# A tiled softmax on one core: unrolled instruction streams against loops with hand-placed semaphores

## The chip, the core and the metric

The kernel runs on one core of a Trainium2 chip. The metric is the device time of one execution in microseconds. Each execution also has a span, from the first to the last recorded instruction; in nearly all runs here the time is 1.7 to 1.8 us longer than the span. The granted clock was 1.0.

## The reference

```python
x = randn(32, 512, 1024) as float32; temperature = 0.5
scaled  = x / temperature
shifted = scaled - max(scaled, axis=-1, keepdims=True)
exp_x   = exp(shifted)
return exp_x / sum(exp_x, axis=-1, keepdims=True)
```

That is 16,384 rows of 1024 numbers. A tile is 128 partitions with 8 rows each, 4 MB, so there are 16 tiles. Everything is read once and written once: 67.11 MB each way.

## The kernel before

Each engine of the core has an instruction stream of its own; the page counts 224 busy instructions of DVE, 257 of ACT and 20 of Pool. SP (SyncE) issues the loads, DVE (VectorE) takes the maximum of a group of four rows and scales it into a bias, ACT (ScalarE) does the exponential and the sum of a row in one instruction of the program (in the trace an ACTIVATE of 1137 ns on the mean and an ACTIVATION_READ_ACCUMULATOR of 186 ns), DVE inverts the sums and multiplies the rows by them, and Pool (GpSimd) issues the store. A tile that was stored frees its buffer, one of six, for a new load. All is unrolled in Python: each engine gets a straight list of instructions, and the framework places the semaphores, the counters by which engines wait for one another. PE (TensorE) has nothing to do.

```python
TILES, BUFS, GROUP = [[8]] * 16, 6, 4
...
def maximum(g):       # DVE
    nc.vector.tensor_reduce(out=top, in_=tiles[i][:, a : a + k, :], axis=X, op=extreme)
    nc.vector.tensor_scalar_mul(bias, in0=top, scalar1=-scale)
def exponential(g):   # ACT, one instruction a row
    for b in range(k):
        nc.scalar.activation(row, row, Exp, bias=bias[:, b : b + 1], scale=scale, accum_out=sums[:, b : b + 1])
def divide(g):        # DVE
    nc.vector.reciprocal(recip, sums)
    for b in range(k):
        nc.vector.tensor_scalar_mul(row, in0=row, scalar1=recip[:, b : b + 1])
def store(g):         # Pool; then the next load, by SP
    nc.gpsimd.dma_start(out=dram(of, i)[...], in_=tiles[i][...])
    load()
...
for g in range(len(groups) + 1):      # a group's division comes after the next group's maximum
    if g < len(groups): maximum(g); exponential(g)
    if g > 0: divide(g - 1); store(g - 1)
```

Of the kernel before, what the change touches and what calls it, by code (L numbers as in the profile page):

```python
# [1 line left out]

# [4 lines left out]



TILES = [[8]] * 16  # L10
BUFS = 6

GROUP = 4


@with_exitstack
def kernel(
    ctx: ExitStack,
    tc: tile.TileContext,
    x: bass.AP,  # L20
    temperature: bass.AP,
    out: bass.AP,
):
    nc = tc.nc
    f32 = mybir.dt.float32
    scale = 1.0 / float(temperature)
    extreme = mybir.AluOpType.max if scale > 0 else mybir.AluOpType.min

    P = 128
    xf = x.flatten_outer_dims()  # L30
    of = out.flatten_outer_dims()
    n, d = xf.shape
    assert sum(sum(ks) for ks in TILES) * P == n

    data = ctx.enter_context(tc.tile_pool(name="data", bufs=BUFS))
    stats = ctx.enter_context(tc.tile_pool(name="stats", bufs=4))


    groups, first, r = [], [], 0
    for i, ks in enumerate(TILES):  # L40
        first.append(r)
        r += sum(ks)
        a = 0
        for k in ks:
            for b in range(0, k, GROUP):
                m = min(GROUP, k - b)
                groups.append((i, a + b, m, (a, k) if b + m == k else None))
            a += k

    def dram(t, i):  # L50
        k = sum(TILES[i])
        block = t[P * first[i] : P * (first[i] + k), :]
        return block.rearrange("(p k) d -> p k d", p=P, k=k)

    tiles, small = [], []

    def load():
        i = len(tiles)
        if i < len(TILES):
            xt = data.tile([P, sum(TILES[i]), d], f32, name="xt")  # L60
            nc.sync.dma_start(out=xt, in_=dram(xf, i))
            tiles.append(xt)

    def maximum(g):
        i, a, k, _ = groups[g]
        top, bias, sums, recip = (
            stats.tile([P, k], f32, name=name) for name in ("top", "bias", "sums", "recip")
        )
        small.append((bias, sums, recip))
        nc.vector.tensor_reduce(  # L70
            out=top, in_=tiles[i][:, a : a + k, :], axis=mybir.AxisListType.X, op=extreme
        )
        nc.vector.tensor_scalar_mul(bias, in0=top, scalar1=-scale)  # L73

    def exponential(g):
        i, a, k, _ = groups[g]
        bias, sums, _ = small[g]
        for b in range(k):
            nc.scalar.activation(  # L79
                tiles[i][:, a + b, :],  # L80
                tiles[i][:, a + b, :],
                mybir.ActivationFunctionType.Exp,
                bias=bias[:, b : b + 1],
                scale=scale,
                accum_out=sums[:, b : b + 1],
            )

    def divide(g):
        i, a, k, _ = groups[g]
        _, sums, recip = small[g]  # L90
        nc.vector.reciprocal(recip, sums)  # L91
        for b in range(k):
            nc.vector.tensor_scalar_mul(  # L93
                tiles[i][:, a + b, :], in0=tiles[i][:, a + b, :], scalar1=recip[:, b : b + 1]
            )

    def store(g):
        i, _, _, part = groups[g]
        if part:
            a, k = part  # L100
            nc.gpsimd.dma_start(out=dram(of, i)[:, a : a + k, :], in_=tiles[i][:, a : a + k, :])  # L101
            if a + k == sum(TILES[i]):
                load()



    with tc.manual_schedule():
        for _ in range(BUFS):
            load()
        for g in range(len(groups) + 1):  # L110
            if g < len(groups):
                maximum(g)
                exponential(g)
            if g > 0:
                divide(g - 1)
                store(g - 1)


# [1 line left out]
_INS = ['x', 'temperature']  # L120
_OUTS = [((32, 512, 1024), 'float32')]

_NUMBERS = {'temperature': 0.5}


# [26 lines left out]
```

## Time and profile before

| | before |
|---|---|
| time, median of 3 runs | 318.3 us (318.11 to 318.39) |
| the profiled run: time, span | 318.68 us, 316.9 us |
| instructions in the trace | 639 |
| DVE, ACT busy | 74%, 47% |
| packets of 32 KB on the DMA engines | 4096, that is 256 on each of 16 |
| instruction fetches of 8 KB inside the span | 4 |
| last byte written; semaphore of the last store; end of the span | 315.06; 315.45; 316.9 us |

How to read it: no compute engine is full, but the sixteen DMA engines are (loads 49.5% and stores 49.1% of their time), so the time of the run is the time of the DMA engine that finishes last (315.06 us) plus what follows it: 1.85 us to the end of the span and 1.8 us outside it.

### The profile page before, as it was taken

How to read it: one execution, taken by the hardware profiler on the slowest of the kernel's cores; microseconds unless marked ns; L12 is line 12 of the kernel's file. 1: busy time of each engine (PE TensorE's matmuls, PEld its weight loads, DVE VectorE, ACT ScalarE, POOL GpSimd, SP SyncE). 2: the span in 40 equal slices, each digit the busy share in tenths (PEclk: the TensorE clock that was granted, in tenths of full speed). 3: DMA queues.
4: the chain of work that ended last, by engine and by line, in shares of the span. 5: the costliest groups of instructions: out<-in, count | busy, mean ns of one | idle time of the engine just before them, and what ended most of it. 6: DMA issues, size and time to landing. Idle time of an engine off the chain costs nothing.

```text
span 316.9 us, 639 instructions
## 1 busy us (share of the span) xinstructions
DVE 235.5 (74%) x224; ACT 149.6 (47%) x257; POOL 8.8 (3%) x20
## 2 busy tenths in 40 slices
DVE  0399999999689494995949869496793967949710
ACT  0176666666526255361554606455163551635500
POOL 0000000000000000000000000000000000000000
DMA  8999999999999999999999999999999999999995
GB/s 331 409 451 414 385 459 422 438 436 422 455 405 455 409 459 405 455 422 438 434 426 451 409 455 411 455 414 447 426 434 435 426 451 409 451 418 447 430 414 232
DMA packets 4612, 134.25 MB, mean 424 GB/s; under 512 B 512, under 2 KB 512, under 8 KB 512
## 3 DMA queue, kind: packets, MB, share of 16 engines
q1 hardware_dynamic: 2304, 67.11, 49.5%
q0 software_dynamic: 2304, 67.11, 49.1%
q14 instruction: 4, 0.03, 0.0%
HBM read 67.11 MB, written 67.11 MB: 424 GB/s over the span
## 4 chain that ended last, share of the span: by engine, by line
issue 89%; DMA 4%; POOL 2%; POOLq 0%
DMA xt<-in_x_dram 4%; POOL out_dram L101 2%; POOLq L147 0%; POOLq L101 0%
## 5 line engine op out<-in xcount | busy, mean ns | idle before, releaser
L79 ACT ACTIVATE xt<-xt,bias 128x1024 f32<-128x1024 f32 x128 | 145.4, 1137 | 136.9 <-DVE recip L91 119.5
L70 DVE TENSOR_REDUCE top<-xt 128x4 f32<-128x4096 f32 x32 | 141.3, 4416 | 62.8 <-DMA xt<-in_x_dram 62.8
L93 DVE TENSOR_SCALAR xt<-xt,recip 128x1024 f32<-128x1024 f32 x128 | 87.7, 749 | 1.1
L79 ACT ACTIVATION_READ_ACCUMULATOR xt<-xt,bias 128x1 f32 x128 | 23.8, 186 | 0.0
L101 POOL DMA_DIRECT2D out_dram<-xt x16 | 8.6, 540 | 294.4 <-DVE xt L93 294.4
L79 ACT ACT_TABLE_LOAD x1 | 1.3, 1283 | 13.2 <-DMA xt<-in_x_dram 13.2
L91 DVE RECIPROCAL recip<-sums 128x4 f32<-128x4 f32 x32 | 5.5, 171 | 2.1 <-ACT xt L79 2.1
L73 DVE TENSOR_SCALAR bias<-top 128x4 f32<-128x4 f32 x32 | 5.4, 170 | 1.1
L133 POOL MEMSET const-float32-0.0<- 128x1 f32 x1 | 0.1, 98 | 0.2 <-issue 0.2
L133 POOL MEMSET const-bfloat16-1.0<- 128x1 bf16 x1 | 0.1, 101 | 0.0
L133 POOL MEMSET const-float32-1.0<- 128x1 f32 x1 | 0.1, 98 | 0.0
L133 POOL MEMSET const-uint8-127<- 128x1 uint8 x1 | 0.1, 98 | 0.0
## 6 DMA issues: line engine op xcount, KB each, us to landing
xt<-in_x_dram SPq DMA_DIRECT2D x16, 4096.0 KB, 50.2
out_dram<-xt POOLq DMA_DIRECT2D x16, 4096.0 KB, 38.4
```

The costliest lines, as they stand in the source:

```text
L70: nc.vector.tensor_reduce(out=top, in_=tiles[i][:, a : a + k, :], axis=mybir.AxisListType.X, op=extreme)
L73: nc.vector.tensor_scalar_mul(bias, in0=top, scalar1=-scale)
L79: nc.scalar.activation(tiles[i][:, a + b, :], tiles[i][:, a + b, :], mybir.ActivationFunctionType.Exp, bias=bias[:, b : b + 1], scale=scal ...
L91: nc.vector.reciprocal(recip, sums)
L93: nc.vector.tensor_scalar_mul(tiles[i][:, a + b, :], in0=tiles[i][:, a + b, :], scalar1=recip[:, b : b + 1])
L101: nc.gpsimd.dma_start(out=dram(of, i)[:, a : a + k, :], in_=tiles[i][:, a : a + k, :])
L133: nc = _bacc.Bacc("TRN2", target_bir_lowering=False, num_devices=1)
```

## The change

The intent was to cut the instruction lists of DVE and ACT to loops that need no fetching, and to tidy up both ends of the run: the first store is held until load 2 has landed, the last store goes by SP, and Pool need not be drained at the end.

```diff
-TILES = [[8]] * 16
-BUFS = 6
+SLOTS, ROWS = 6, 8
-GROUP = 4
+GROUPS = [4, 2, 2]
 ... (one ring of six slots in place of six tiles, one semaphore each for loaded and stored per slot)
+    def take(engine, sem, count=1):
+        engine.wait_ge(sem, count).then_inc(sem, -count)
 ...
+        for i in range(tiles):
+            nc.tensor.wait_ge(loaded[i % SLOTS], 16 * (i // SLOTS + 1)).then_inc(ready, 1)
+        nc.gpsimd.wait_ge(loaded[2], 16)
+        for i in range(tiles - 1):
+            nc.gpsimd.wait_ge(scaled, len(groups) * (i + 1))
+            nc.gpsimd.dma_start(out=dram(of, i), in_=slot(i)).then_inc(stored[i % SLOTS], 16)
+        with nc.vector.Fori(0, tiles) as t:
+            first = t % SLOTS * ROWS
+            take(nc.vector, ready)
+            for a, k in groups:          # all maxima of the tile
+                ... tensor_reduce, take(topped), tensor_scalar_mul, then_inc(biased, k)
+            for a, k in groups:          # then all its divisions
+                take(nc.vector, summed, k)
+                ... reciprocal, take(inverted), k products, then_inc(scaled, 1)
+        with nc.scalar.Fori(0, tiles) as t:
+            ... take(biased) at a group's first row; activation per row, then_inc(summed, 1)
+        nc.sync.wait_ge(scaled, len(groups) * tiles)
+        nc.sync.dma_start(out=dram(of, tiles - 1), in_=slot(tiles - 1)).then_inc(finished, 16)
 ... (both sections without the drain of Pool)
```

PE, which is idle otherwise, turns "load i has landed" into one counter, `ready`, for the loop of DVE. Since a loop's addresses depend on `t`, each row's instruction is preceded by a register step (128 on DVE and 128 on ACT), and each wait is an instruction of its own that also counts the semaphore down (160 on DVE, 48 on ACT). A first small activation (`warm`) makes ACT load its table earlier than at 13.2 us.

More of the change, by code (lines that the diff above doesn't have):

```diff
@@ L32 @@
     n, d = xf.shape
-    assert sum(sum(ks) for ks in TILES) * P == n
-    data = ctx.enter_context(tc.tile_pool(name="data", bufs=BUFS))
-    stats = ctx.enter_context(tc.tile_pool(name="stats", bufs=4))
-    groups, first, r = [], [], 0
-    for i, ks in enumerate(TILES):
-        first.append(r)
-        r += sum(ks)
-        a = 0
-        for k in ks:
-            for b in range(0, k, GROUP):
-                m = min(GROUP, k - b)
-                groups.append((i, a + b, m, (a, k) if b + m == k else None))
-            a += k
@@ L50, in dram @@
-    def dram(t, i):
-        k = sum(TILES[i])
-        block = t[P * first[i] : P * (first[i] + k), :]
-        return block.rearrange("(p k) d -> p k d", p=P, k=k)
-    tiles, small = [], []
-    def load():
-        i = len(tiles)
-        if i < len(TILES):
-            xt = data.tile([P, sum(TILES[i]), d], f32, name="xt")
-            nc.sync.dma_start(out=xt, in_=dram(xf, i))
-            tiles.append(xt)
-    def maximum(g):
-        i, a, k, _ = groups[g]
-        top, bias, sums, recip = (
-            stats.tile([P, k], f32, name=name) for name in ("top", "bias", "sums", "recip")
-        )
-        small.append((bias, sums, recip))
-        nc.vector.tensor_reduce(
-            out=top, in_=tiles[i][:, a : a + k, :], axis=mybir.AxisListType.X, op=extreme
-        )
-        nc.vector.tensor_scalar_mul(bias, in0=top, scalar1=-scale)
@@ L75, in exponential @@
-    def exponential(g):
-        i, a, k, _ = groups[g]
-        bias, sums, _ = small[g]
-        for b in range(k):
-            nc.scalar.activation(
-                tiles[i][:, a + b, :],
-                tiles[i][:, a + b, :],
-                mybir.ActivationFunctionType.Exp,
-                bias=bias[:, b : b + 1],
-                scale=scale,
-                accum_out=sums[:, b : b + 1],
-            )
-    def divide(g):
-        i, a, k, _ = groups[g]
-        _, sums, recip = small[g]
-        nc.vector.reciprocal(recip, sums)
-        for b in range(k):
-            nc.vector.tensor_scalar_mul(
-                tiles[i][:, a + b, :], in0=tiles[i][:, a + b, :], scalar1=recip[:, b : b + 1]
-            )
@@ L97, in store @@
-    def store(g):
-        i, _, _, part = groups[g]
-        if part:
-            a, k = part
-            nc.gpsimd.dma_start(out=dram(of, i)[:, a : a + k, :], in_=tiles[i][:, a : a + k, :])
-            if a + k == sum(TILES[i]):
-                load()
-    with tc.manual_schedule():
-        for _ in range(BUFS):
-            load()
-        for g in range(len(groups) + 1):
-            if g < len(groups):
-                maximum(g)
-                exponential(g)
-            if g > 0:
-                divide(g - 1)
-                store(g - 1)
+    tiles = n // (P * ROWS)
@@ new lines @@
+    assert tiles * P * ROWS == n and sum(GROUPS) == ROWS
+    groups = [(sum(GROUPS[:g]), k) for g, k in enumerate(GROUPS)]
+    of_group = dict(groups)
+    pool = ctx.enter_context(tc.tile_pool(name="data", bufs=1))
+    ring = pool.tile([P, SLOTS * ROWS, d], f32, name="ring")
+    top = pool.tile([P, ROWS], f32, name="top")
+    bias = pool.tile([P, ROWS], f32, name="bias")
+    sums = pool.tile([P, ROWS], f32, name="sums")
+    recip = pool.tile([P, ROWS], f32, name="recip")
+    warm = pool.tile([P, 1], f32, name="warm")
@@ new lines, with slot @@
+    loaded = [tc.alloc_semaphore(f"loaded{s}") for s in range(SLOTS)]
+    stored = [tc.alloc_semaphore(f"stored{s}") for s in range(SLOTS)]
+    ready, topped, biased, summed, inverted, scaled, finished = (
+        tc.alloc_semaphore(name)
+        for name in ("ready", "topped", "biased", "summed", "inverted", "scaled", "finished")
+    )
+    def dram(t, i):
+        return t[P * ROWS * i : P * ROWS * (i + 1), :].rearrange("(p k) d -> p k d", p=P, k=ROWS)
+    def slot(i):
+        s = i % SLOTS
+        return ring[:, ROWS * s : ROWS * (s + 1), :]
@@ new lines, in take @@
+    def take(engine, sem, count=1):
+        engine.wait_ge(sem, count).then_inc(sem, -count)
+    with tc.tile_critical(no_gpsimd_drain=True):
+        for i in range(tiles):
+            if i >= SLOTS:
+                nc.sync.wait_ge(stored[i % SLOTS], 16 * (i // SLOTS))
+            nc.sync.dma_start(out=slot(i), in_=dram(xf, i)).then_inc(loaded[i % SLOTS], 16)
+        for i in range(tiles):
+            nc.tensor.wait_ge(loaded[i % SLOTS], 16 * (i // SLOTS + 1)).then_inc(ready, 1)
[7 more added lines that the diff above has]
+            for a, k in groups:
+                nc.vector.tensor_reduce(
+                    out=top[:, a : a + k],
+                    in_=ring[:, bass.ds(first + a, k), :],
+                    axis=mybir.AxisListType.X,
+                    op=extreme,
+                ).then_inc(topped, 1)
+                take(nc.vector, topped)
+                nc.vector.tensor_scalar_mul(
+                    bias[:, a : a + k], in0=top[:, a : a + k], scalar1=-scale
+                ).then_inc(biased, k)
+            for a, k in groups:
+                take(nc.vector, summed, k)
+                nc.vector.reciprocal(
+                    recip[:, a : a + k], sums[:, a : a + k]
+                ).then_inc(inverted, 1)
+                take(nc.vector, inverted)
+                for b in range(a, a + k):
+                    row = ring[:, bass.ds(first + b, 1), :]
+                    ins = nc.vector.tensor_scalar_mul(row, in0=row, scalar1=recip[:, b : b + 1])
+                ins.then_inc(scaled, 1)
+        nc.scalar.activation(
+            warm, nc.const_aps.tensor(0.0, (P, 1)), mybir.ActivationFunctionType.Exp
+        )
+        with nc.scalar.Fori(0, tiles) as t:
+            first = t % SLOTS * ROWS
+            for b in range(ROWS):
+                row = ring[:, bass.ds(first + b, 1), :]
+                if b in of_group:
+                    take(nc.scalar, biased, of_group[b])
+                nc.scalar.activation(
+                    row,
+                    row,
+                    mybir.ActivationFunctionType.Exp,
+                    bias=bias[:, b : b + 1],
+                    scale=scale,
+                    accum_out=sums[:, b : b + 1],
+                ).then_inc(summed, 1)
+        i = tiles - 1
+        nc.sync.wait_ge(scaled, len(groups) * tiles)
+        nc.sync.dma_start(out=dram(of, i), in_=slot(i)).then_inc(finished, 16)
+        for i in range(tiles - SLOTS, tiles - 1):
+            nc.sync.wait_ge(stored[i % SLOTS], 16 * (i // SLOTS + 1))
@@ L120 @@
+    with tc.tile_critical(no_gpsimd_drain=True):
+        nc.sync.wait_ge(finished, 16, synchronizes=[nc.sync.lower_ap(slot(tiles - 1))])
 _INS = ['x', 'temperature']
```

## The prediction

> **What bounds the kernel now.** I read the page first: engines, DMA row, queues.
>
> ```profile
> span 316.9 us, 639 instructions
> DVE 235.5 (74%) x224; ACT 149.6 (47%) x257; POOL 8.8 (3%) x20
> ...
> DMA  8999999999999999999999999999999999999995
> ...
> q1 hardware_dynamic: 2304, 67.11, 49.5%
> q0 software_dynamic: 2304, 67.11, 49.1%
> q14 instruction: 4, 0.03, 0.0%
> ```
>
> No compute engine is full; the sixteen DMA engines are, in every slice but the first and the last: 49.5% + 49.1% of their time is packets of loads and stores. The trace's list of packets says how one engine spends its time: 16 loads and 16 stores of 4 MB are 4096 packets of 32 KB, 256 for each engine, and the usual packet takes 1.213 us. So an engine needs 256 x 1.213 = 310.5 us (16 x 32768 B / 1.213 us = 432 GB/s), and the first packet starts at 1.74 us. What can be won is only what an engine loses beside its 310.5 us, ahead of it and behind it.
>
> Then the end, in the view by windows (us, DVE, ACT, POOL, clock, DMA share, GB/s), the timeline and the view of the closing source line:
>
> ```profile
> 302.00:303.00 1.00, 0.60 (x1) 0.00 (x0) 0.10 (x1) 1.00 1.21 524
> 303.00:304.00 1.00, 0.00 (x0) 0.00 (x0) 0.43 (x1) 1.00 0.16 66
> 304.00:305.00 1.00, 0.00 (x0) 0.00 (x0) 0.00 (x0) 1.00 1.14 492
> ...
> 312.00:313.00 1.00, 0.00 (x0) 0.00 (x0) 0.00 (x0) 1.00 1.22 524
> 313.00:314.00 1.00, 0.00 (x0) 0.00 (x0) 0.00 (x0) 1.00 0.08 33
> 314.00:315.00 1.00, 0.00 (x0) 0.00 (x0) 0.00 (x0) 1.00 0.00 0
> ```
>
> ```profile
> 282.87 4.42 DVE L70 TENSOR_REDUCE top<-xt 128x4 f32<-128x4096 f32 x1 [4.48 <-DMA xt<-in_x_dram]
> ...
> 302.90 0.53 POOL L101 DMA_DIRECT2D out_dram<-xt  x1 [11.72 <-DVE xt L93]
> ```
>
> ```profile
> L147 SPq EVENT_SEMAPHORE  x11: 17/28/28, 315.5 to 316.8; - x11
> ...
> L147 POOLq DRAIN  x3: 34/101/13271, 302.9 to 316.6; - x3
> ```
>
> Two things stand there. Around 303.5 us most engines have finished store 14 and stand still up to 0.7 us, since the last store is issued at 302.90 and its first packet starts at 303.99. And a packet is counted where it starts: 33 GB/s in 313 to 314 is one packet of 32 KB, of one engine. Fifteen engines end by 314.2; this one starts its last packet at 313.84 and ends at 315.06. The store's semaphore is complete at 315.45, and the barriers take 1.46 us more, to 316.905. The late engine had no gap at 303: its last packet of store 14 ran to 305.38. So **the end is set by one engine that is behind the others**, and an earlier last store alone doesn't help it.
>
> Why is it behind? After each load's last packet every engine writes a 4-byte semaphore, and for one load to the next these lie 19.36 us apart, the same to 0.05 us on nearly every engine. The last engine's are 20.02 us apart twice: from 48.67 to 68.69 and from 223.63 to 243.65, +0.66 us each. The four packets of 8 KB on q14, instruction fetches, start at 64.4, 65.0, 193.9 and 241.8 us. Another engine loses some 0.5 us across the one at 193.9. The ACT waits carry the same mark:
>
> ```profile
> ACT xt L79 <- issue: 8.3, 3, 2.8
> ```
>
> [...] while both queues have work, a load takes 19.36 us, twice the 9.7 us that 8 packets take alone. [...] Here the fetch is hidden from ACT but costs its DMA engine 0.5 to 0.7 us. Whether a loop fetches again, no trace here shows. [...] Here 1.09 us for the last store by Pool, and 1.00 us for the first load by SP, so I count no gain from the path itself.
>
> **The change, part by part.**
>
> *Loops.* By the list of the built instructions the DVE program goes from 242 to 52 and ACT's from 177 (more as executed: the page counts 257 busy ones, since each activation also reads its accumulator) to 38. Both loops fit well inside what was fetched before the start, so the four fetches should go. The late engine gets 2 x 0.66 = 1.32 us back: its store 14 ends at 305.38 - 1.32 = 304.06 instead. The others finished store 14 between 303.3 and 304.15 (their semaphores). Eight more packets without a gap, 8 x 1.213 = 9.7 us, put the last byte at 313.0 to 313.8. I take 313.7 for the last, against 315.06: **-1.35 us**.
>
> *Order on DVE.* All maxima of a tile now come before its divisions, in groups 4, 2, 2. From a tile's landing: reduces 2 x 4.416 = 8.8 with three small operations 9.4 us. ACT starts at 4.6 and at 1.13 us a row has four rows at 9.3 and all eight at 13.9. DVE then has reciprocal and four products (0.66 apart) to 12.4, two rows to 14.0, the last two to 15.6. With semaphore hops and address registers I say 16.2 us, an estimate from these rows. Before, the last tile took 282.87 to 302.60, 19.7 us. So the last store is ready at 299.1, ahead of the 303.3 where the engines run dry: the gap at 303 goes. This is worth nothing added to the above; it is what keeps the other fifteen from becoming the new last ones (with the gap they end at 313.74 to 313.9). In the steady part DVE's 16.2 is under the 19.36 of DMA per tile.
>
> *First store waits for load 2.* Tile 0 is ready near 13.1 + 16.2 = 29.3, load 2 lands at 32.48; before, the first store went at 33.10. So it is issued 0.5 us earlier than before, which shifts the mix of loads and stores, not their sum: 0.
>
> *Last store by SP, and no Pool drain.* Pool's drain stood from 302.88 to 316.15, that is 0.70 us past the landing, but SP itself needed eight semaphore waits and two drains from 315.46 to 316.08, so the drain held up the barrier by 0.07 us. In the new program SP has about seven steps of 0.06 us after its wait on the last store, most other waits being done while the store runs. From landing to end 1.2 us instead of 1.46: **-0.25 us**.
>
> *Start.* One more hop between engines before SP's first load, some three steps: **+0.15 us**.
>
> Sum: -1.35 - 0.25 + 0.15 = -1.45; 318.3 - 1.45 = 316.85, say **316.8 us**.
>
> **Rivals.** (a) *The loops fetch at every jump back.* Fetches of 8 KB at 0.66 us of one engine, 16 rounds for DVE and ACT each: if they all hit one DMA engine, +10 to +20 us; spread evenly +1 to +2. [...] Against: the loop bodies are 38 and 22 instructions, and what stood resident at the start of before served at least 64 us. It would make 319 to 330. (b) *DVE becomes the bound.* Each dynamic address adds a register instruction (8 per tile and engine) and the semaphores are taken by instructions of their own, some 20 per tile on DVE. Slack is 19.36 - 16.2 = 3.2 us, so they would need 160 ns each, unhidden; the semaphore steps in the closing barrier lie 60 ns apart. Then 16 x the excess comes on top; at 200 ns each, +13 us. I think it unlikely. (c) *The lag comes back from elsewhere.* Packets of 1.5 to 2.4 us at the start and of 1.8 us around 36 us, where stores begin, are in both kernels; if the late engine's place came from them, only the end's 0.25 is left: 318.0. (d) *More is won*, because other engines' times at 303 hide losses too: the least conceivable is 1.74 + 0.8 for the slow first packet + 310.5 + 0.4 to the semaphore + 1.0 + 1.4 (318.3 - 316.9, time outside the span) = 315.8.
>
> **Range and chances.** Point (d) is nearly a floor, so faster by over 2% (under 311.9) is out of reach: 0.01. (c) gives the upper end of what I expect, 318.2. (a) and (b) together have 0.04 to pass 324.7. The rest, 0.95, is within 2%. Range 315.8 to 318.3.
>
> **What would show it.** q14 with no packets inside the span; every engine's load semaphores 19.36 us apart throughout; no window of low GB/s near 303; the last packets of all engines within some 0.9 us of each other, ending by 313.9; the last store issued by SP near 299; landing to end about 1.2 us. I am wrong if q14 still has packets (a), if DVE waits no longer for loads (b), or if one engine still ends a packet late without any fetch (c).

No term of the sum is among them: it stands at -1.35 - 0.25 + 0.15 = -1.45 and 316.85 us. Point (d) takes it that the steady part can't get faster; that is not shown. Of the 4096 packets of 32 KB none took less than 1.211 us, before or after. The 1.09 us of Pool's last store and the 1.00 us of SP's first load run from issue to first packet. Rival (a): against it, and for the step on loops, the trace of before has seven fetches of 8 KB on q14 between 10.5 and 7.4 us before the span and none from there to 64.4 us, when it has 47 instructions of DVE and 64 of ACT. And the 0.15 us for the start was an estimate.

## The result, and the profile after

| | before | after |
|---|---|---|
| median of 6 runs each, in the same rounds | 318.24 us (318.11 to 318.39) | 318.31 us (318.10 to 318.82) |
| ratio after / before, 95% interval | | 1.0005 (0.9992 to 1.0017): same |
| the profiled run: time, span | 318.68, 316.9 us | 318.14, 316.4 us |
| instructions in the trace | 639 | 1208 |
| 8 KB fetches inside the span | 4 | none |
| last byte; store's semaphore; end of span | 315.06; 315.45; 316.9 | 314.58; 315.06; 316.4 us |

A ratio is the mean time of one kernel's fast runs over the mean of the other's of the same rounds, so it is not quite the ratio of the medians quoted. The change moved nothing: the predicted 1.45 us did not come, and the median is just outside the range's upper end of 318.3.

The page of the changed kernel, in the parts that the prediction quoted of before (engines, DMA row, queues):

```profile
span 316.4 us, 1208 instructions
DVE 244.4 (77%) x272; ACT 148.1 (47%) x258; POOL 8.3 (3%) x19
...
DMA  8999999999999999999999999999999999999995
...
q1 hardware_dynamic: 2448, 71.30, 52.7%
q0 software_dynamic: 2160, 62.92, 46.1%
```

There is no line any more for q14, the queue of the instruction fetches: they are gone. The DMA row has not changed in a single digit. And the count of instructions has nearly doubled, though the programs became shorter. Of the 569 more, 354 are register steps and branches that a loop executes in every round (a_unrolled, below, has 854 without them); the rest are mostly the waits placed by hand and the smaller groups. The view by source line shows the waits alone, for the helper `take`:

```profile
L63 DVEq EVENT_SEMAPHORE  x160: 21/21/21, 13.4 to 296.7; - x160
L63 ACTq EVENT_SEMAPHORE  x48: 17/17/17, 18.5 to 291.9; - x48
```

These cost DVE and ACT almost nothing (21 and 17 ns each). The view of instruction groups says the same: before its maxima DVE still waits 39.4 us in all, for loads.

```profile
L84 DVE TENSOR_REDUCE top<-ring 128x2 f32 (+1 forms) x48 | 143.8, 2996 | 39.4 <-DVEq L63 39.4
```

The timeline of the last tile (start, duration, engine, line), and the view by windows (us, DVE, ACT, POOL, clock, DMA share, GB/s) of the end:

```profile
281.98 4.42 DVE L84 TENSOR_REDUCE top<-ring 128x4 f32 x1 [3.17 <-DVEq L63]
...
296.77 1.41 DVE L102 TENSOR_SCALAR ring<-ring,recip  x2 [0.15 <-DVEq L63]
298.21 0.35 SPq L127 DMA_DIRECT2D out_dram<-ring  x1
```

```profile
302.00:303.00 1.00, 0.00 (x0) 0.00 (x0) 0.00 (x0) 1.00 1.21 524
303.00:304.00 1.00, 0.00 (x0) 0.00 (x0) 0.00 (x0) 1.00 0.99 426
304.00:305.00 1.00, 0.00 (x0) 0.00 (x0) 0.00 (x0) 1.00 0.99 426
...
312.00:313.00 1.00, 0.00 (x0) 0.00 (x0) 0.00 (x0) 1.00 1.21 524
313.00:314.00 1.00, 0.00 (x0) 0.00 (x0) 0.00 (x0) 1.00 0.08 33
314.00:315.00 1.00, 0.00 (x0) 0.00 (x0) 0.00 (x0) 1.00 0.00 0
```

The last tile takes 281.98 to 298.18, 16.2 us instead of 19.7; the last store is issued at 298.21 rather than 302.90; the stretch of 66 GB/s near 303 is filled, at 426. (That stretch was in the one profile that the prediction had; b_again, below, doesn't have it in the kernel before either.) All of this is as it should be. But the row 313 to 314 is the same as before: one packet of 32 KB starts there, of one engine, when the others are done. **A single late DMA engine ends this run too, and there was no fetch that could have made it late.**

The closing source line of the changed kernel:

```profile
L162 SPq EVENT_SEMAPHORE  x5: 17/28/5303, 309.7 to 316.3; - x5
...
L162 POOLq DRAIN  x3: 34/107/1286, 309.3 to 316.1; - x3
```

SP has 5 semaphore steps there instead of 11; its long one, 5.3 us, is the wait for the last store. From the semaphore of the store to the end of the span it is now 1.31 us instead of 1.46.

### The profile page after: what moved, and what is told of

Same layout as the page of the kernel before. It is cut to its first block, busy times and chain, and to the rows that moved or that the text cites. A ratio compares the mean times of both kernels' runs of the same rounds, so it can differ in the third digit from the quotient of the medians.

```text
span 316.4 us, 1208 instructions
## 1 busy us (share of the span) xinstructions
DVE 244.4 (77%) x272; ACT 148.1 (47%) x258; POOL 8.3 (3%) x19
## 5 line engine op out<-in xcount | busy, mean ns | idle before, releaser
L115 ACT ACTIVATE ring<-ring,bias x128 | 145.1, 1135 | 147.1 <-ACTq L63 147.1
L84 DVE TENSOR_REDUCE top<-ring 128x2 f32 (+1 forms) x48 | 143.8, 2996 | 39.4 <-DVEq L63 39.4
L102 DVE TENSOR_SCALAR ring<-ring,recip x128 | 89.1, 749 | 7.2 <-DVEq L63 1.8
L115 ACT ACTIVATION_READ_ACCUMULATOR ring<-ring,bias 128x1 f32 x128 | 24.0, 187 | 0.0
L78 POOL DMA_DIRECT2D out_dram<-ring x15 | 8.1, 542 | 271.1 <-DVE ring L102 238.5
L91 DVE TENSOR_SCALAR bias<-top 128x2 f32<-128x2 f32 (+1 forms) x48 | 8.2, 170 | 7.2
L96 DVE RECIPROCAL recip<-sums 128x2 f32<-128x2 f32 (+1 forms) x48 | 7.9, 164 | 0.0
```

The lines of the kernel that those rows point to most:

```text
L78: nc.gpsimd.dma_start(out=dram(of, i), in_=slot(i)).then_inc(stored[i % SLOTS], 16)
L84: nc.vector.tensor_reduce(out=top[:, a : a + k], in_=ring[:, bass.ds(first + a, k), :], axis=mybir.AxisListType.X, op=extreme,).then_inc(t ...
L91: nc.vector.tensor_scalar_mul(bias[:, a : a + k], in0=top[:, a : a + k], scalar1=-scale).then_inc(biased, k)
L96: nc.vector.reciprocal(recip[:, a : a + k], sums[:, a : a + k]).then_inc(inverted, 1)
L102: ins = nc.vector.tensor_scalar_mul(row, in0=row, scalar1=recip[:, b : b + 1])
L115: nc.scalar.activation(row, row, mybir.ActivationFunctionType.Exp, bias=bias[:, b : b + 1], scale=scale, accum_out=sums[:, b : b + 1],).th ...
```

## Where the lag comes from: one number per tile

The page doesn't tell the engines apart. The trace's list of packets does, in one way. After each load's last packet every DMA engine writes a 4-byte semaphore (256 packets of 4 bytes on q1 in the trace of before, 16 for each of 16 loads). In the steady part these are 19.36 us apart for an engine that loses nothing (16 packets of 1.210 us). So for each load to the next, sixteen steps can be paired up, and what is over 19.36 is what that engine lost in that tile. Paired that way from 67 to 260 us, the profiled runs show this (us per tile; "one" is the engine that loses most over these tiles apart from the fetches; in brackets the start of the step with the fetch, us):

```text
                     instr. in trace  one loses, by tile                        mean    fetches of 8 KB, loss of the engine hit
before                     639        0 .05 .04 .03 .04 .05 .03 .05 .04 .05 .04  0.04    .52 (183), .66 (222), two more near 65
before, run again          639        0 .03 .06 .06 .04 .03 .06 .06 .05 .05 .04  0.04    .64 (183), .73 (221), two more near 65
after                     1208        .13 .12 .09 .11 .11 .08 .09 .10 .11 .09 .14  0.10  none
after, run again          1208        .13 .09 .18 .14 .14 .16 .14 .11 .12 .13 .10  0.13  none
```

In the kernel before one engine loses next to nothing steadily, and the fetches cost whole steps to whichever engine serves them. In the changed kernel there is no such step, but one and the same engine loses tile after tile, 0.10 us on the mean and 0.13 in the rerun (in the first of these profiles another engine lost 0.13 and 0.14 in two single tiles). Over the 14 tiles from 46 us to the end that is 0.06 to 0.09 x 14 = 0.8 to 1.3 us more than before. Fifteen engines of the changed kernel do end early, at 313.2 to 314.21; the sixteenth ends at 314.58 in the profile, and in its rerun at 315.35 with the others at 313.2 to 314.06. So without this one engine the two runs would have ended 0.4 and 1.3 us sooner.

My theory after the result was therefore: the loops did save the fetches, and something in the changed kernel makes one DMA engine lose steadily. The candidates were the new order on DVE, the earlier stores, the last store by SP, and the number of executed instructions. The experiments take them in turn. "Before" kernels start from the kernel before, "after" kernels from the changed one.

## The experiments

All seventeen gave the right result. Ratios are to runs of the kernel before on the same chip.

### Both kernels again (b_again, a_again)

No edit.

> The kernel before, unchanged: noise, and a second trace of it. Theory F (the fetches set the end, and the profiled run of before, 318.68 us against a median of 318.24, happened to have two of them on its late engine): ratio 1.000 within 0.0015; the four instruction fetches are there again, but they fall on other engines, and in a run near 318.2 the last byte ends near 314.6 to 314.8 rather than 315.06. Rival R (lateness comes from the start and from the stretch where stores begin, fetches hardly matter): the fetches may even hit the late engine again with the time near 318.2.

> The changed kernel, unchanged: a second trace and the noise of its ratio. Ratio 1.000 within 0.0015. Theory R expects the engines that end last to differ from the first trace's, with the last byte 312.4 to 313.1 us after the first packet, as chance in the first 40 us has it, and no packet of q14.

Measured: before 318.33 us, ratio 1.0005 (0.9991 to 1.0018), after 318.55 us, ratio 1.0004 (0.9990 to 1.0017), 5 runs each. The profiled run of before has its four fetches at 65.1, 65.1, 192.7 and 240.1 us and a last byte at 314.62; its late engine was hit twice again. The last tile was done earlier than in the first profile, so that Pool issued the last store at 301.23 instead of 302.90, and the gap at 303 isn't there:

```profile
301.23 0.53 POOL L101 DMA_DIRECT2D out_dram<-xt  x1 [11.72 <-DVE xt L93]
...
303.00:304.00 1.00, 0.00 (x0) 0.00 (x0) 0.00 (x0) 1.00 1.22 524
```

What follows: the result holds, and the two lags are of two kinds, as in the table above.

### Without the loops (a_unrolled)

```diff
@@ -79,3 +79,3 @@
 
-        with nc.vector.Fori(0, tiles) as t:
+        for t in range(tiles):
             first = t % SLOTS * ROWS
@@ -108,3 +108,3 @@
         )
-        with nc.scalar.Fori(0, tiles) as t:
+        for t in range(tiles):
             first = t % SLOTS * ROWS
```

> The changed kernel with both loops unrolled, nothing else altered: instruction fetches come back on q14 (3 to 5 packets of 8 KB). Theory F: slower than the changed kernel by 0.5 to 1.3 us (ratio to before about 1.002 to 1.004). Rival R: within 0.3 us of the changed kernel, since four fetches seldom hit the engine that ends last.

Measured: 319.86 us (319.69 to 320.09), ratio 1.0052 (1.0038 to 1.0065). The page of this run:

```profile
span 317.8 us, 854 instructions
...
q14 instruction: 5, 0.04, 0.0%
```

Five fetches are back, and the engines they hit lose 0.43 to 0.68 us each. The last byte is at 316.13, with fifteen engines done by 314.64. So the loops are worth 319.86 - 318.55 = 1.3 us, close to the predicted 1.35. But only half of it is what the prediction meant: the spans have a median of 317.5 against 316.8 us, so 0.7 us lie inside the span. The other 0.6 us lie outside (time less span is 2.4 us here and 1.8 in the rerun of the changed kernel), where the trace has one more 8 KB fetch, at 319.8 us. The kernel before, unrolled as well, has no such part, so this isn't the price of unrolling in general; and a_old_order, below, has such a fetch at 317.33 with 1.8 us outside, so a late fetch alone doesn't explain it. It stays open.

The pairing of load semaphores shows more in this trace. Beside what the fetches cost, one engine loses 0.07 to 0.20 us in every tile from 67 to 282 us, 0.11 on the mean, and others lose in single tiles. **So the steady loss is there without the loops, too, with 854 instructions in the trace: the 354 register steps and branches of the loops are not needed for it.**

### The wait for load 2 (a_nowait, a_wait3, a_late)

```diff
@@ -74,3 +74,2 @@
 
-        nc.gpsimd.wait_ge(loaded[2], 16)
         for i in range(tiles - 1):
```

> The changed kernel without the first store's wait for load 2: the first store is issued near 30 us instead of 33.05. Theory N (the wait is worth nothing, the sum of bytes is the same): within 0.3 us of the changed kernel. Rival W (a store that begins while only the loads' first packets are under way costs its engine more, or the last load lands too late for the last store): 0.5 to 2 us slower.

Measured: 323.62 us (322.99 to 324.99), ratio 1.0182 (1.0163 to 1.0201), the largest effect of any single line of the change. The timelines of Pool's first issues, of the changed kernel and then without the wait, and after each the page's packet line:

```profile
33.05 0.67 POOL L78 DMA_DIRECT2D out_dram<-ring  x1 [32.61 <-DMA ring<-in_x_dram]
...
DMA packets 4608, 134.22 MB, mean 424 GB/s; under 512 B 512, under 2 KB 512, under 8 KB 512
```

```profile
30.22 0.67 POOL L77 DMA_DIRECT2D out_dram<-ring  x1 [29.78 <-DVE ring L101]
...
DMA packets 4608, 134.22 MB, mean 418 GB/s; under 512 B 512, under 2 KB 512, under 8 KB 512
```

The first store goes 2.8 us earlier, and the mean falls from 424 to 418 GB/s. In the list of packets, those that took over 1.24 us are 5 after 40 us and before 283 us in the changed kernel, but 239 here, spread over the whole run. So what the start of the stores sets lasts; that it is the offset between the streams of loads and stores is my reading. The wait is no gain over before, whose first store went at 33.1 by itself because its tile took longer; it is what keeps the faster tile of the changed kernel from spoiling the rest.

```diff
@@ -74,3 +74,3 @@
 
-        nc.gpsimd.wait_ge(loaded[2], 16)
+        nc.gpsimd.wait_ge(loaded[3], 16)
         for i in range(tiles - 1):
```

> The first store waits for load 3 instead of load 2, so it begins about one load (9.7 us) later. Without the wait it began 2.8 us earlier and the kernel was 5.4 us slower. Theory B (what counts is where in a load the stores begin, a boundary between loads being good): 318.4 within 0.5, with few load packets over 1.29 us after 45 us. Rival E (early starts are bad, late ones are good or neutral): the same time, or faster; rival T (only this one moment is good): 320 or more.

Measured: 319.51 us (319.27 to 319.55), ratio 1.0037 (1.0020 to 1.0053). The first store is issued at 42.7 us. After the transition, some 32 packets near 45 us, hardly any are long (12 over 1.24 us from 100 to 283 us): this first store, at 42.7 us instead of 33.05, did the streams no lasting harm. The last byte is at 314.83, no later than usual; the 1.2 us over the changed kernel come at the end, where the span goes on for 2.9 us after the last byte instead of 1.8. There store 14, by Pool, is the last to land, at 315.31.

```diff
@@ -76,3 +76,3 @@
         for i in range(tiles - 1):
-            nc.gpsimd.wait_ge(scaled, len(groups) * (i + 1))
+            nc.gpsimd.wait_ge(scaled, len(groups) * (i + 1) + (i > 0))
             nc.gpsimd.dma_start(out=dram(of, i), in_=slot(i)).then_inc(stored[i % SLOTS], 16)
```

> The changed kernel, but every store from the second on also waits until the first group of the next tile is divided, some 12 us later, so that stores stand less deep in Pool's queue (issue to landing near 37 us instead of 50). Theory O (issue times): 316.8 to 317.5. Rival S: 318.4 within 0.3.

Measured: six runs from 318.99 to 334.86 us, median 324.35, three of them counted as slow for being more than 1.5% above the fastest (the clock was 1.0 in all six); the three fast ones (318.99, 321.31 and 323.0) give a ratio of 1.006 (1.0032 to 1.0089). Holding each later store until the next tile has begun to be divided issued the second one at 59.2 us instead of 46.3, and after 100 us it has 214 packets over 1.24 us, as without the wait. So the second store, at 46 us, is not too early in the changed kernel: putting it off makes things worse. In both bad cases a load lands 2 to 4 us from the nearest landing of a store, in the good ones 7 to 10 us; no run shows why that matters.

### The order on DVE (a_old_order)

```diff
 GROUPS = [4, 2, 2] -> [4, 4]
+        take(nc.vector, ready)                         # tile 0 outside the loop
+        maximum(0, a0, k0); maximum(0, a1, k1); divide(0, a0, k0)
+        with nc.vector.Fori(1, tiles) as t:
+            take(nc.vector, ready)
+            maximum(first, a0, k0)
+            divide(last, a1, k1)                       # of the tile before, as in the kernel before
+            maximum(first, a1, k1)
+            divide(first, a0, k0)
+        divide((tiles - 1) % SLOTS * ROWS, a1, k1)
```

> The loops alone, nearly: the changed kernel with the DVE order of before (groups of 4 and 4, maxima of one tile between the divisions of the last), still looped, still the last store by SP. The unrolled changed kernel was 1.4 us slower than the looped one, so the loops are worth what was predicted, and something else in the change takes as much. Theory O (the new DVE order takes it, by issuing stores at other times, after which single DMA engines run at 1.216 us a packet instead of 1.210): 316.8 to 317.3, ratio 0.996 to 0.997. Rival S (it is the start hop and the last store by SP, or chance): within 0.3 us of the changed kernel's 318.4.

Measured: 318.46 us (318.45 to 318.97), ratio 1.0012 (0.9999 to 1.0025), with 1115 instructions in the trace. One engine loses 0.10 to 0.16 us per tile and ends at 314.89; fifteen end at 313.15 to 313.68. So the order on DVE is not what holds the engine back: that theory falls. The last store is issued at 301.20 here and at 298.21 in the changed kernel, and the times are the same: an earlier last store is worth nothing.

### Who issues the last store (a_pool_last, b_sp_last)

```diff
@@ -125,4 +125,4 @@
         i = tiles - 1
-        nc.sync.wait_ge(scaled, len(groups) * tiles)
-        nc.sync.dma_start(out=dram(of, i), in_=slot(i)).then_inc(finished, 16)
+        nc.gpsimd.wait_ge(scaled, len(groups) * tiles)
+        nc.gpsimd.dma_start(out=dram(of, i), in_=slot(i)).then_inc(finished, 16)
         for i in range(tiles - SLOTS, tiles - 1):
```

> The changed kernel with its last store issued by Pool instead of SP, at the same time near 298. Theory L (a last store in the loads' queue goes round by round beside store 14 and lets single engines fall behind; all stores in one queue avoid it): 317.6 or less. Theory O and chance: within 0.3 us of 318.4; the wait for Pool's drain is hidden since Pool is drained by the closing barrier anyway, at most +0.2.

Measured: 318.67 us (318.43 to 318.90), ratio 1.0015 (1.0002 to 1.0028). One engine loses 0.08 to 0.15 us per tile here, too.

```diff
@@ -100,3 +100,4 @@
             a, k = part
-            nc.gpsimd.dma_start(out=dram(of, i)[:, a : a + k, :], in_=tiles[i][:, a : a + k, :])
+            queue = nc.sync if g == len(groups) - 1 else nc.gpsimd
+            queue.dma_start(out=dram(of, i)[:, a : a + k, :], in_=tiles[i][:, a : a + k, :])
             if a + k == sum(TILES[i]):
```

> The kernel before with its last store by SP, nothing else. My prediction's step (an earlier first packet of the last store doesn't help, as the last engine has no gap there; Pool's drain holds the end by under 0.1 us): ratio 1.000 within 0.001. Rival D (Pool's drain and its slower path cost 0.5 us or more): ratio 0.998 or less.

Measured: 318.03 us (317.88 to 318.29), ratio 0.9993 (0.9980 to 1.0006). The timeline of this run has the store on SP at 301.19, which is 1.7 us ahead of Pool's 302.90 in the first profile of before, but only 0.04 ahead of Pool's 301.23 in b_again. So this run changes who issues the store, and hardly when:

```profile
301.19 0.35 SPq L102 DMA_DIRECT2D out_dram<-xt  x1
```

In both directions the effect is within some 0.3 us: who issues the last store is worth next to nothing.

### Fewer and more executed instructions (a_lean, a_spin, a_spin_sem, a_spin8, a_spin20)

What was left was the number of executed instructions, though a_unrolled says already that the number alone can't be all: it loses 0.11 us per tile with 854 of them. First fewer:

```diff
 GROUPS = [4, 2, 2] -> [4, 4]
-                take(nc.vector, summed, k)
+                take(nc.vector, summed)
 ... (ACT raises summed at the last row of a group only, not at each row)
```

> The changed kernel with fewer instructions and semaphore updates: groups of 4 and 4 instead of 4, 2, 2, and ACT raises its semaphore once a group instead of once a row. About 8 instructions and 10 updates a tile fewer of 75. Theory I or U: the one engine loses 0.01 to 0.03 us less per tile, 0.2 to 0.4 us in all: 318.0 to 318.2. Rival P: any value within 0.4 of 318.4.

Measured: 318.47 us (318.06 to 318.81), ratio 1.0003 (0.9986 to 1.0019); 1096 instructions, and one engine loses 0.09 to 0.13 us per tile, 0.11 on the mean, so not less than in the changed kernel. 112 instructions fewer were too small a dose to be seen in the time: inconclusive. Then many more, on PE, which only waits here:

```diff
             nc.tensor.wait_ge(loaded[i % SLOTS], ...).then_inc(ready, 1)
+            with nc.tensor.Fori(0, 40):
+                for _ in range(4):
+                    nc.tensor.wait_ge(loaded[i % SLOTS], 16 * (i // SLOTS + 1))     # already true
```

> In every traced run one DMA engine loses time steadily, tile after tile: 0.03 to 0.07 us in before (639 instructions in the trace), 0.08 to 0.18 us in the looped kernels (1115 to 1208). Here the idle PE runs a loop of 40 rounds of 4 satisfied waits per tile (some 3800 more executed instructions, no data touched, no fetches, since it loops). Theory I (the loss goes with the number of executed instructions or of the records that the trace keeps of them): the one engine loses 0.3 us or more per tile, and the kernel is 3 us or more slower. Rival P (the loss has to do with the phases of the DMA engines and not with instructions): 318.4 within 0.3.

> The same loop on PE, but its four waits come as two pairs that raise and lower a semaphore, so as many instructions again with 160 semaphore updates a tile. Theory U (the loss goes with semaphore updates, 1004 recorded in before and 1405 in the changed kernel): clearly slower than a_spin, by 1 us or more. Theory I: as a_spin within 0.5 us. Rival P: 318.4 within 0.3.

(a_spin_sem has, in place of the four waits, two pairs of a wait that raises a semaphore and one that lowers it.) Measured: 396.25 us and 646.47 us. Both were mis-sized and inconclusive: PE needed 23.4 and 39 us for a tile's rounds, more than the 19.36 of DMA, and since it passes on `ready` it became the bound. The same loops with 8 and with 20 rounds leave PE idle for 40% of a tile or more:

```diff
@@ -72,2 +72,5 @@
             nc.tensor.wait_ge(loaded[i % SLOTS], 16 * (i // SLOTS + 1)).then_inc(ready, 1)
+            with nc.tensor.Fori(0, 8):
+                for _ in range(4):
+                    nc.tensor.wait_ge(loaded[i % SLOTS], 16 * (i // SLOTS + 1))
 
```

> The changed kernel, PE in addition executes 8 rounds of 4 satisfied waits per tile in a loop (in the first try 40 rounds took PE 23 us a tile and made it the bound, so that run said nothing of the time; 8 rounds should take under 5 us). About 32 more executed instructions a tile beside some 75. Theory I (executed instructions, or their records, slow the stores of one DMA engine): that engine loses 0.13 to 0.17 us a tile instead of 0.11 to 0.13; 318.7 to 319.2. Rival P (nothing to do with instructions): 318.4 within 0.3.

> As a_spin8 with 20 rounds, about 81 more executed instructions a tile, PE busy some 12 us of a tile's 19.4, no fetches inside the run. Theory I: the one engine loses 0.17 to 0.25 us a tile, its slow packets lie where PE's loop runs; 319.2 to 320.5, and more than a_spin8. Rival P: 318.4 within 0.3, as a_spin8.

Measured: 319.06 us (318.86 to 319.16), ratio 1.0025 (1.0011 to 1.0039) with 8 rounds, and 319.95 us (319.72 to 320.06), ratio 1.0052 (1.0038 to 1.0065) with 20 rounds. The view by windows of the end, first with 8 rounds, then with 20:

```profile
312.00:313.00 1.00, 0.00 (x0) 0.00 (x0) 0.00 (x0) 1.00 1.14 492
313.00:314.00 1.00, 0.00 (x0) 0.00 (x0) 0.00 (x0) 1.00 0.09 33
314.00:315.00 1.00, 0.00 (x0) 0.00 (x0) 0.00 (x0) 1.00 0.08 33
315.00:316.00 1.00, 0.00 (x0) 0.00 (x0) 0.00 (x0) 1.00 0.00 0
```

```profile
312.00:313.00 1.00, 0.00 (x0) 0.00 (x0) 0.00 (x0) 1.00 1.21 524
313.00:314.00 1.00, 0.00 (x0) 0.00 (x0) 0.00 (x0) 1.00 0.01 0
314.00:315.00 1.00, 0.00 (x0) 0.00 (x0) 0.00 (x0) 1.00 0.08 33
315.00:316.00 1.00, 0.00 (x0) 0.00 (x0) 0.00 (x0) 1.00 0.08 33
```

One packet a window, after the others are done: in the changed kernel it starts in 313 to 314, with 8 rounds there is another in 314 to 315, with 20 rounds another in 315 to 316. Fifteen engines end where they did (313.4 to 313.8 and 313.5 to 313.9), the one at 315.51 and 316.44:

```text
                 instr. in trace   one loses, by tile                            mean   last byte   time
after                1208      .13 .12 .09 .11 .11 .08 .09 .10 .11 .09 .14       0.10    314.58   318.31
8 rounds on PE       1736      .17 .13 .17 .18 .16 .16 .15 .14 .16 .14 .17       0.16    315.51   319.06
20 rounds on PE      2504      .23 .16 .24 .18 .19 .23 .21 .22 .22 .21 .20       0.21    316.44   319.95
```

This is a response to the dose: 528 and 1296 more instructions in the trace made the run 0.75 and 1.64 us longer than the changed kernel, 1.3 to 1.4 ns each, though they touch no data and nobody waits for them.

### The same dose in the kernel before (b_spin, b_spin_long, b_nops)

One doubt stayed: the doses were semaphore waits, in the kernel with the ring and its own semaphores. So the kernel before got a loop on PE without any wait:

```diff
@@ -106,2 +106,6 @@
 
+    with tc.tile_critical(no_gpsimd_drain=True):
+        with nc.tensor.Fori(0, 400):
+            for _ in range(4):
+                nc.tensor.nop()
     with tc.manual_schedule():
```

> The kernel before, with nothing changed but that PE, which has no work in it, runs a loop of 400 rounds of four empty instructions from the start (some 2400 more executed instructions, no wait, no data). Theory I (executed instructions hold back one DMA engine, at the 1.2 us per 1000 that the two doses in the changed kernel gave): 2.9 us more on one engine while PE loops; seen in the time as 2.9 if it is also the engine the fetches hit, 1.5 or more if it is another: 319.7 to 321.2. Rival X (the steady loss comes with something else of the changed kernel, its ring in one buffer, its own semaphores, its address registers, and the spin loops only added waits on semaphores): no effect, 318.2 within 0.3, and no engine that loses more than 0.05 us per tile outside the fetches.

Measured: 318.25 us, ratio 1.0001 (0.9988 to 1.0015). The time missed the expectation of 319.7 or more. But the view by source line shows why this dose was smaller than planned: PE's loop has only its register step and its branch in the trace, the four empty instructions are not there, and it was through at 160 us.

```profile
L108 PEldq ALU_OP  x400: 36/36/42, 13.4 to 160.1; - x134
L108 PEldq COMPARE_BRANCH  x400: 76/208/227, 13.6 to 160.2; - x134
```

And the loss per tile follows that loop. While it runs, one engine loses 0.18, 0.16, 0.18, 0.17 and 0.16 us; from the tile after, 0.04, 0.04, 0.06, 0.06, 0.04 and 0.03. The rival, no engine over 0.05, falls. The time didn't move since another engine, hit by two fetches, ended later (315.37 in that run). Hence two more, one with 800 rounds, which covers the run, and one with 200 rounds of twenty empty instructions:

```diff
-        with nc.tensor.Fori(0, 400):
+        with nc.tensor.Fori(0, 800):     # b_spin_long
```

> The kernel before with PE's empty loop at 800 rounds instead of 400, which at 0.368 us a round covers the span to 308 us instead of 160. With 400 rounds one engine lost 0.16 to 0.18 us per tile while the loop ran and 0.03 to 0.06 after it, but another engine, hit by two fetches, ended later, so that the time did not move. Theory I: the loss of 0.17 per tile now goes on to the end; that engine loses 14 x 0.17 = 2.4 us, ends near 313.3 + 2.4 = 315.7 if it started with the first ones, and sets the end: 318.7 to 319.8. Rival Y (the loss belongs to the first half of the run, not to the loop): 318.2, and the loss drops to 0.05 again after some 150 us.

```diff
-        with nc.tensor.Fori(0, 400):
-            for _ in range(4):
+        with nc.tensor.Fori(0, 200):     # b_nops
+            for _ in range(20):
```

> As with 400 rounds of four empty instructions, but 200 rounds of twenty. The trace records the branch and the register step of a round and not its empty instructions, so that a round has 2 records and 22 executed instructions instead of 2 and 6. If a round of twenty takes 0.9 to 1.1 us, a tile's 19.4 us hold some 40 records and 430 executed instructions, against 105 and 315 with four. Theory R (the loss follows the records): 0.045 + 0.05 = about 0.09 us per tile on the one engine. Theory E (it follows executed instructions): 0.045 + 0.13 x 430 / 315 = about 0.22. The time is 318.2 to 318.6 with R and up to 319.6 with E.

Measured: 319.16 us (319.06 to 319.4), ratio 1.0034 (1.0020 to 1.0048) with 800 rounds; 318.16 us, ratio 0.9999 (0.9985 to 1.0013) with 200. The two loops by source line and, for 800 rounds, the end by windows:

```profile
L108 PEldq ALU_OP  x800: 36/36/42, 13.5 to 307.2; - x160
...
313.00:314.00 1.00, 0.00 (x0) 0.00 (x0) 0.00 (x0) 1.00 0.16 66
314.00:315.00 1.00, 0.00 (x0) 0.00 (x0) 0.00 (x0) 1.00 0.08 33
```

```profile
L108 PEldq ALU_OP  x200: 36/36/42, 13.6 to 86.7; - x100
```

With 800 rounds the loss, 0.14 to 0.20 us per tile (mean 0.16), goes on to the end. That engine ends at 315.36, 0.8 us after any other (314.55 for one that a fetch hit), and the time is 1.1 us longer than that of the kernel before in the same rounds. With 200 rounds the loss is 0.19 in the one tile from 66 us on, 0.08 in the one that holds the loop's end at 86.7, and 0.03 to 0.05 from then on. So **the same kernel, with the same data, semaphores and addresses, has a DMA engine that loses 0.16 us per tile while an idle engine turns an empty loop, and 0.04 when it doesn't; two loops that end at 87 and 160 us take the loss with them, and one that runs to 307 us keeps it**. That shows that executed instructions, or the records that the trace keeps of them, can make such a loss. For the changed kernel it is argued and not shown, and the doses don't match: PE's empty loop puts 105 instructions into a tile for 0.12 us, 1.1 ns each, the changed kernel has 36 more than before for 0.06 to 0.09 us, 1.7 to 2.5 ns each, and the changed kernel without loops has 13 more for 0.07 us, some 5 ns each. So what the two have in common, and not the loops, brings most of their loss. Perhaps kinds of instructions count differently. Semaphore updates are no better measure: the traces have 1004 of them before, 1405 after, 1408 without loops, but 1181 in a_lean for the same 0.11 us. No run takes the kinds apart. The second question of b_nops, whether records or executed instructions count, was not answered: a round takes 0.368 us with twenty empty instructions as with four, so they are not executed, or at no cost that shows; if they are not executed, the two theories don't differ here.

## Why the prediction was wrong

Its frame was right: the time is the slowest DMA engine plus both ends, and the change couldn't move it by 2%. These steps held, or missed without deciding the result:

- *The fetches go.* No q14 line; sixteen rounds of loops of 38 and 22 instructions, and no 8 KB fetch inside the span at any jump back, so rival (a) is out, and unrolling again brings five fetches. Their worth of 1.35 us came out as 1.3 us in a_unrolled, though half of that by an extra outside the span that I had not thought of.
- *Order on DVE.* 16.2 us were said and measured for the last tile; the last store was to be ready at 299.1 and was issued at 298.21. There is no gap at 303, but b_again has none either, and an earlier last store is worth nothing, as a_old_order shows. Rival (b) is out: DVE waits 39.4 us for loads.
- *First store.* It went at 33.05, only 0.05 us earlier than before and not 0.5, and is no gain. But the "0" hides that a_nowait is 5 us slower (323.62 us against 318.55 of a_again); I saw the wait as harmless where it is needed.
- *Three readings were wrong without deciding anything.* The three waits of ACT on "issue" end at 44.79, 59.56 and 74.34 and last 2.7 to 2.8 us, as do their neighbours that are put down to DVE (2.76), so they are no mark of the fetches. One of the "others" finished store 14 at 304.49 and not by 304.15; fetches had hit it twice, too (0.54 and 0.52 us), and it ended at 314.18. And packets follow one another at 19.36 / 16 = 1.210 us, so 256 take 309.8 us and not 310.5, which puts the floor of (d) 0.7 lower.
- *Both ends.* The closing steps gave -0.15 instead of -0.25 us, the start +0.2 instead of +0.15: the first load is issued at 0.95 instead of 0.74 (and its first packet starts 1.01 us later, where it was 1.00), as the two timelines show, first before and then after:

```profile
0.74 2.89 SPq L61 DMA_DIRECT2D xt<-in_x_dram  x6
```

```profile
0.95 2.94 SPq L70 DMA_DIRECT2D ring<-in_x_dram  x6
```

**The step that failed** is in the part on loops: "Eight more packets without a gap, 8 x 1.213 = 9.7 us, put the last byte at 313.0 to 313.8. I take 313.7 for the last, against 315.06". It takes for granted that an engine without fetches keeps pace with the others. Fifteen did, but for single losses of 0.13 and 0.14 us. One lost 0.10 to 0.13 us per tile with no fetch in the run, against 0.04 before, and that took back what the fetches had cost. The change adds 569 executed instructions to the 639 in the trace, 36 a tile, and the doses on PE show that executed instructions, or their records, can hold one engine back (0.16 and 0.21 us per tile against 0.10; 0.16 against 0.04 in the kernel before). I had priced these instructions only where they run, on DVE and ACT, where they cost nothing, and not on the DMA engines. Which part of the change makes the loss stays open: a_unrolled rules out that the loops' own instructions are needed for it, a_old_order the order on DVE, a_pool_last the last store by SP. Rival (c), "the lag comes back from elsewhere", at 318.0, is the one that came, but the place I named for it, the packets of the start, isn't it.

The size, from the terms of the prediction and the median run: its sum amounts to a last byte at 313.85 with the start, 0.39 us to the semaphore, 1.21 to the end and 1.4 outside the span, 316.85 in all. The changed kernel's profile has 0.48, 1.31 and 318.14 - 316.37 = 1.77, which leaves 318.31 - 3.56 = 314.75 for the last byte of a median run. So of the 1.46 us missing, 0.9 is a later last byte, 0.2 the end, and 0.37 a baseline taken from two runs: I had subtracted the span of a profiled run (of 318.68 us) from the median of others (318.3), and called the 1.4 the time outside the span, where 318.68 - 316.9 = 1.8 was to be had from one run. The 0.9 is inferred, since no median run was traced, and not all of it is the steady loss: the next engines end at 314.21 and 314.06 in the two traces, 0.2 to 0.4 us after the 313.85 of the sum.

What else stays open: whether the instructions themselves hold back the engine or the trace's records of them. Every run here, the timed ones too, has a span and so was recorded. If it is the records, part of this loss may exist only while one measures; no run here decides it. Nor do the runs say which of the sixteen engines it is, why it is one, or why certain offsets between loads and stores slow the packets.

No version beat both kernels: b_sp_last is lowest at 318.03 us, but its interval holds 1.

## What to carry to other kernels

Here the DMA engines were full (98.6% of the span before), and the last of them set the time: one ended 0.4 to 1.5 us after the other fifteen in before, after, its rerun and a_unrolled. So where they are full, look at each engine's own lag, and ask of every part of a change what it does to that one: here a fetch of 8 KB cost the engine it fell to 0.43 to 0.73 us (before, its rerun and a_unrolled), and a loop on the otherwise idle PE a steady trickle of 1.1 to 1.4 ns for each instruction in the trace (b_spin_long, a_spin8, a_spin20). Here the loops removed the fetches, and something in the kernel around them brought a trickle of the same size that stayed when the loops were unrolled again. So undo each half of such a change alone, and read each engine's lag there too, before laying a loss to one of them. And take a baseline's parts from one run, not from two.
